# Values of the dilated groups projected with stationary weights and turned on TensorE

## The chip, the cores and the metric

The kernel runs on one core of one Trainium2 chip. The metric is the device time of one execution in microseconds (us), lower being better. Before the change it is 2150.77 us, the median of three runs (2149.27 to 2153.36).

## What is computed

The reference is a decoder trunk of two layers over 512 tokens of width 1024, all in float32. Each layer projects its input x once, runs three attention mixers (A: three groups of heads with dilated windows, B: a sliding window, C: latent attention), gates and merges them, and closes with a feed-forward part. The change concerns mixer A alone. Cut to it:

```
proj  = x @ w_in                          # x: 512 x 1024
a_qkv = proj[:, :4608].reshape(512, 3 groups, 3 (q, k, v), 8 heads, 64)
groups (window, dilation): (128, 1), (512, 4), (2048, 16)
for each group:
    tokens are regrouped by residue t mod dilation; within a residue
    each query attends to the keys of its causal band:
    p = softmax(q @ k.T / 8 + bias[distance])
    o = p @ v
o_a = the groups' outputs, weighted by their softmax denominators
```

Groups 1 and 2 are the dilated ones. The kernel sorts the tokens of both by residue modulo 4 (group 2's dilation of 16 is left to its bias table, which masks what is not a multiple of 16 apart), so four blocks of 128 tokens, one for each residue, take the place of the four blocks of 128 neighbours.

## The kernel before

Products are made from split numbers: every operand stands as a high and a low float32r part, and a product takes three matmuls into one bank (`mm3`, L170 to L173). The input stands transposed, as xT (xh, xl): model width on the partitions in eight chunks, the 512 tokens along the columns.

Mixer A of a layer is done in six jobs, `A_JOBS` = (0,0), (0,1), (0,2), (1,1), (1,2), (1,0): a half of the heads and a group. `project_a` makes a job's values, then for each of two pairs of heads (c) the query and the key projection: `o1` (L339) keeps 128 weight columns stationary and streams all 512 tokens, 8 chunks x 3 = 24 matmuls of 512 columns into a bank qkp. ACT copies the high part out and DVE subtracts it for the low part (`split_to`, L175). For a dilated group the copy regroups the columns by residue, and the key goes into a block-diagonal pair kh, kl, whose zero halves POOL sets (`block_diagonal`, L535). After each pair of heads four items of attention (one for a block of 128 queries) join the queue of `att`.

An item runs in three steps, each put into the program when `gap` finds that it is time for one: scores (scp), transposing the probabilities on TensorE (ptp, then pT), and values (op); its result goes by a row tile and a DMA issued on POOL to arow. `gap(time)` is called by the projections as they go on, and adds to a budget in proportion to the work left; the budget is capped at 4.

Values of the dilated groups come from `values_far` (L607), called in the job of group 1 for groups 1 and 2 of that half together: the stationary operand is every fourth token of xT, the moving one 512 weight columns (256 of either group), four residues into four banks at a time, three of tag mm and the only one of tag o; op uses that one too. All 96 matmuls stand before the first copy out; then four copies fill four slots vv, kept for both jobs, and one `gap(4 * UNIT)` follows.

Banks: three of tag mm (projections), two pt (transposes), two sc (scores), one o. Slots: the pool sp has 22 tiles of 4 KB a partition, shared by latT (three), vv, bias, q, kh, kl, pT, ct and others. Weights come through `Weights`: loads on the SP queue four ahead, splits (whi on ACT, wlo on DVE) two ahead. Within these rules a scheduler of the framework sets the order of the instructions on each engine when the program is built; an engine runs its own in that order, and a tile is taken when its last reader is through.

Of the kernel before, what the change touches and what calls it, by code (L numbers as in the profile page):

```python
# [12 lines left out]
F32 = mybir.dt.float32  # L13
F32R = mybir.dt.float32r
AF = mybir.ActivationFunctionType
# [5 lines left out]
P = 128  # L21
D = 1024
S = 512
KT = D // P
# [8 lines left out]
UNIT = 24 * 0.218  # L33
# [10 lines left out]
def dap(base, offset, dims):  # L44
    return bass.AP(tensor=base.tensor, offset=base.offset + offset, ap=[list(d) for d in dims])
# [88 lines left out]
def hybrid_trunk(ctx: ExitStack, tc: tile.TileContext, I, out):  # L134
    nc = tc.nc
# [13 lines left out]
    def mm_bank(name):  # L149
        return bank("mm", 3, name)  # L150

    def pt_bank(name):
        return bank("pt", 2, name)
# [4 lines left out]
    def o_bank(name):  # L158
        return bank("o", 1, name)
# [7 lines left out]
    def slot(name, dtype=F32):  # L167
        return sp.tile([P, 1024], dtype, name=name, tag="s")

    def mm3(o, lh, ll, rh, rl, start, stop):  # L170
        nc.tensor.matmul(o, lh, rh, start=start, stop=False)  # L171
        nc.tensor.matmul(o, lh, rl, start=False, stop=False)  # L172
        nc.tensor.matmul(o, ll, rh, start=False, stop=stop)  # L173

    def split_to(hi, lo, src, scale=None):  # L175
        if scale is None:
            nc.scalar.activation(hi, src, AF.Copy)  # L177
            nc.vector.tensor_tensor(lo, src, hi.bitcast(F32), ALU.subtract)  # L178
        else:
            nc.scalar.activation(hi, src, AF.Copy, scale=scale)  # L180
            nc.vector.scalar_tensor_tensor(lo, src, scale, hi.bitcast(F32), op0=ALU.mult, op1=ALU.subtract)  # L181


    specs = []
# [14 lines left out]
    def plan(l):  # L199
        w_in, r_in = I["w_in"], l * D  # L200

        def win(key, c0, n, k0=0, kts=KT, pool=None):
            col_chunk((l, key), w_in, r_in, D_IN, c0, n, k0=k0, kts=kts, pool=pool)

        for k in range(0, KT, 2):
            win(("lat", k), COL_CQ, 416, k, 2, sp if k < 4 else None)
        for j, (hf, g) in enumerate(A_JOBS):
            c0 = g * 1536 + hf * 256
            if g == 0:
                for k in (0, 4):  # L210
                    win((j, "v", k), c0 + 1024, 256, k, 4)
            elif g == 1:
                for k in range(0, KT, 2):
                    src = dap(w_in, r_in * D_IN + k * P * D_IN + c0 + 1024,
                              [[D_IN, P], [P * D_IN, 2], [1536, 2], [1, 256]])
                    pieces = [((lambda r, a=a: r.rearrange("p (k g n) -> p k g n", k=2, g=2)[:, a]), src[:, a])
                              for a in range(2)]
                    specs.append(((l, (j, "v", k)), 1024, pieces, None))
            for c in range(2):
                for nm, o in (("q", 0), ("k", 512)):  # L220
                    win((j, nm, c), c0 + o + c * P, P)
        win("bk", COL_BKV, P)
        win("bv", COL_BKV + P, P)
        for i in range(4):
            pieces = []
            for kv in range(2):
                src = dap(w_in, r_in * D_IN + COL_B + kv * 256 + i * 64, [[D_IN, P], [P * D_IN, KT], [1, 64]])
                pieces.append((lambda r, o=kv * 64: r.rearrange("p (k n) -> p k n", k=KT)[:, :, o:o + 64], src))
            specs.append(((l, "bq", i), 1024, pieces, None))
        for n in range(len(GATES) + GATE_LEAD):  # L230
            if n < len(GATES):
                i, f = GATES[n]
                win(("g", i, f), COL_G + i * D + f * P, P)
            if n >= GATE_LEAD:
                i, f = GATES[n - GATE_LEAD]
                if f % 2 == 0:
                    if i != 1:
                        col_chunk((l, "br", i, f), I["w_branch"], (l * 3 + i) * 512, D, f * P, 256, kts=4)
                        continue
                    pieces = []  # L240
                    for h in range(2):
                        src = dap(I["w_branch"], ((l * 3 + i) * 512 + h * 256) * D + f * P,
                                  [[D, 64], [64 * D, 4], [1, 256]])
                        pieces.append((lambda r, o=h * 64: r[o:o + 64].rearrange("p (k n) -> p k n", k=4), src))
                    specs.append(((l, "br", i, f), 1024, pieces, None))
        for c in range(2):
            for k in range(0, KT, 2):
                col_chunk((l, "wo", c, k), I["w_out"], l * D, D, c * 512, 512, k0=k, kts=2, pool=sp if c else None)
        for h0, h1 in HALVES:
            for f in range(h0, h1):  # L250
                col_chunk((l, "ug", f), I["w_ffn_up"], l * D, N_UP, f * P, P)
                col_chunk((l, "uv", f), I["w_ffn_up"], l * D, N_UP, D_FF + f * P, P)
            for c in range(2):
                for k in range(h0, h1, 2):
                    col_chunk((l, "dn", c, k), I["w_ffn_down"], l * D_FF, D, c * 512, 512, k0=k,
                              kts=min(2, h1 - k), pool=sp if (h1, c) == (KF, 1) and k >= h1 - 3 else None)
# [119 lines left out]
    for l in range(DEPTH):  # L376
# [172 lines left out]
        class JobA:  # L549
# [3 lines left out]
            def __init__(self, hf, g, c, bv, vv):  # L553
                self.hf, self.g, self.c, self.bv, self.vv = hf, g, c, bv, vv
                self.joint = g > 0
                self.vt, self.vh = (1, (g - 1) * 4 + 2 * c) if g else (2, 2 * c)

            def normalize(self, item, n):
                pass
# [47 lines left out]
        def values_far(l, j):  # L607


            pv = [mm_bank("vp") if r < 3 else o_bank("vp") for r in range(4)]  # L610
            for k in range(0, KT, 2):
                w = W.next((l, (j, "v", k)), 2, 512)
                for r in range(4):
                    for kk in range(2):
                        mm3(pv[r], xT[0][:, k + kk, r::4], xT[1][:, k + kk, r::4], w[0][:, kk, :], w[1][:, kk, :],
                            k + kk == 0, k + kk == KT - 1)
            vv = []
            for r in range(4):
                v = slot("vv", F32R).rearrange("p (h a d) -> p h a d", h=8, a=2)
                split_to(v[:, :, 0, :], v[:, :, 1, :], pv[r].rearrange("p (h d) -> p h d", h=8))  # L620
                vv.append(v[:, None])
            gap(4 * UNIT)
            return vv

        far = {}

        def project_a(l, j):

            hf, g = A_JOBS[j]
            if g == 0:  # L630
                vv = values_near(l, j)
            else:
                if g == 1:
                    far[hf] = values_far(l, j)
                vv = far[hf]
            if not tabs:
                make_tables()
            if j == 0:
# [462 lines left out]
```

## Time and profile before

| | |
|---|---|
| median of three runs | 2150.77 us (2149.27 to 2153.36) |
| profiled execution, its own time | 2152.71 us |
| its span, first to last instruction | 2151.0 us |
| TensorE (PE) busy | 2099.3 us, 98% |
| weight loads (PEld) | 1776.0 us, 83% |
| VectorE (DVE) | 1201.9 us, 56% |
| ScalarE (ACT) | 882.6 us, 41% |
| GpSimd (POOL) | 185.5 us, 9% |
| DMA | 220.32 MB, mean 102 GB/s |

Busy shares of TensorE are no measure of its pace: matmuls are pipelined, one that starts each 0.23 us is shown as lasting 0.39. The pace is read from the starts of neighbours in the timeline, and a slow stretch from idle time and from the granted clock. A layer takes half the span, and in each the dilated jobs follow the latent projections (from about 75 to 280 us in layer 0).

### The profile page before, as it was taken

The page shows a single profiled execution, that of the slowest core. Times are in us where ns is not written, and L with a number is a line of the kernel's source. Part 1 is how long each engine was busy: PE and PEld are TensorE (multiplying, and loading weights), DVE is VectorE, ACT ScalarE, POOL GpSimd, SP SyncE. Part 2 cuts the span into 40 slices and gives each one's busy share as a digit, 9 for nine tenths or more (in the row PEclk, how much of TensorE's full clock was granted, in tenths as well). Part 3 has the DMA queues.
Part 4 walks back from the last instruction along what each step waited for, and adds up shares of the span by engine and source line. Part 5 has one row for each costly group of instructions (what it writes and reads, how often), then busy time and mean ns, then how long its engine had stood idle before and what let it go on. Part 6 is the DMA issues. An engine that isn't in the chain of part 4 may idle for free. (4 is left out here: it accounts for less than half of the span.)

```text
span 2151.0 us, 29542 instructions
## 1 busy us (share of the span) xinstructions
PE 2099.3 (98%) x11074; PEld 1776.0 (83%) x11074; DVE 1201.9 (56%) x2585; ACT 882.6 (41%) x1874; POOL 185.5 (9%) x333
## 2 busy tenths in 40 slices
PE   8999999999999999999999989999999999999997
PEld 7888787788888888888888878878888888888886
DVE  4354556766646664366453546566665466644655
ACT  4343444555433343244233434445554324433431
POOL 1021211110000100000020212011010000000001
PEclk9999899999999999999999989999999999999999
DMA  6632433323236233333333233442222352333321
GB/s 183 201 89 82 121 93 116 87 68 97 62 111 195 69 98 93 103 98 93 117 110 87 85 86 106 100 126 77 74 76 76 109 185 73 95 95 101 98 93 64
DMA packets 291467, 220.32 MB, mean 102 GB/s; under 512 B 27914, under 2 KB 265435, under 8 KB 290812
## 3 DMA queue, kind: packets, MB, share of 16 engines
q1 hardware_dynamic: 284860, 203.55, 32.7%
q0 software_dynamic: 6464, 14.89, 2.3%
q8 instruction: 87, 1.43, 0.3%
q14 instruction: 56, 0.46, 0.1%
HBM read 201.38 MB, written 22.26 MB: 104 GB/s over the span
## 5 line engine op out<-in xcount | busy, mean ns | idle before, releaser
L77 DVE TENSOR_TENSOR wlo<-wraw,whi 128x1024 fp32r<-128x1024 f32 (+2 forms) x316 | 380.0, 1204 | 431.6 <-ACT whi L76 429.1
L76 ACT ACTIVATE whi<-wraw 128x1024 fp32r<-128x1024 f32 (+2 forms) x316 | 329.0, 1044 | 454.2 <-PE dnp L172 119.0
L172 PE MATMUL up<-xl,whi 128*128 128x512 f32 (+1 forms) x768 | 285.3, 372 | 0.4
L171 PE MATMUL up<-xh,whi 128*128 128x512 f32 (+1 forms) x768 | 284.2, 372 | 0.7 <-ACT xh L328 0.5
L173 PE MATMUL up<-xh,wlo 128*128 128x512 f32 (+1 forms) x768 | 284.5, 371 | 0.0
L171 PE MATMUL qkp<-xh,whi 128*128 128x512 f32 x464 | 188.3, 406 | 6.8 <-DVE q L181 6.7
L173 PE MATMUL qkp<-xh,wlo 128*128 128x512 f32 x464 | 187.3, 404 | 0.0
L172 PE MATMUL qkp<-xl,whi 128*128 128x512 f32 x464 | 187.3, 404 | 0.0
L171 PEld LDWEIGHTS up<-xh,whi 128*128 128x128 f32 x768 | 144.0, 188 | 26.7 <-ACT xh L328 1.6
L172 PEld LDWEIGHTS up<-xl,whi 128*128 128x128 f32 x768 | 144.7, 188 | 25.9 <-DVE xl L333 1.2
L173 PEld LDWEIGHTS up<-xh,wlo 128*128 128x128 f32 x768 | 144.5, 188 | 24.9
L171 PE MATMUL gp<-xh,whi 128*128 128x512 f32 x384 | 154.7, 403 | 0.7 <-ACT gs L886 0.7
L172 PE MATMUL gp<-xl,whi 128*128 128x512 f32 x384 | 153.2, 399 | 0.0
L173 PE MATMUL gp<-xh,wlo 128*128 128x512 f32 x384 | 152.2, 396 | 0.0
L493 ACT ACTIVATE sb<-sb,row 128x128 f32<-128x128 f32 (+1 forms) x192 | 81.0, 422 | 140.1 <-DVE row L490 134.1
L172 PE MATMUL dnp<-wlo,hT 128*128 128x512 f32 x352 | 136.9, 389 | 0.0
L173 PE MATMUL dnp<-whi,hT 128*128 128x512 f32 x352 | 136.8, 389 | 0.0
L171 PE MATMUL dnp<-whi,hT 128*128 128x512 f32 x352 | 135.6, 389 | 0.0
L177 ACT ACTIVATE pT<-ptp 128x512 fp32r<-128x512 f32 (+1 forms) x176 | 82.0, 477 | 116.3 <-PE ptp L504 114.7
L178 DVE TENSOR_TENSOR pT<-ptp,pT 128x512 fp32r<-128x512 f32 (+1 forms) x176 | 93.6, 540 | 53.1 <-ACT pT L177 52.5
L490 DVE CUSTOM_DVE_ANT_0 sb<-scp,bias 128x128 f32<-128x128 f32 (+1 forms) x192 | 55.7, 320 | 116.7 <-DMA arow<-row 98.7
L171 PEld LDWEIGHTS qkp<-xh,whi 128*128 128x128 f32 x464 | 89.4, 193 | 24.0 <-DVE q L181 7.9
(301 smaller groups left out, 4354.1 us busy)
## 6 DMA issues: line engine op xcount, KB each, us to landing
wraw<-in_w_in_dram SPq DMA_DIRECT2D x108, 512.0 KB, 4.0
wraw<-in_w_ffn_up_dram SPq DMA_DIRECT2D x88, 512.0 KB, 4.0
wraw<-in_w_ffn_down_dram SPq DMA_DIRECT2D x40, 512.0 KB, 3.8
wraw<-in_w_in_dram SPq DMA_DIRECT2D x48, 256.0 KB, 3.6
wraw<-in_w_branch_dram SPq DMA_DIRECT2D x16, 512.0 KB, 3.5
wraw<-in_w_out_dram SPq DMA_DIRECT2D x16, 512.0 KB, 6.7
arow<-row POOLq DMA_DIRECT2D x96, 66.0 KB, 1.9
ct<-arow SPq DMA_DIRECT2D x16, 396.0 KB, 3.5
```

Of the source, the lines that this page charges most:

```text
L76: nc.scalar.activation(hi[:, :n], raw[:, :n], AF.Copy)
L77: nc.vector.tensor_tensor(lo[:, :n], raw[:, :n], hi[:, :n].bitcast(F32), ALU.subtract)
L171: nc.tensor.matmul(o, lh, rh, start=start, stop=False)
L172: nc.tensor.matmul(o, lh, rl, start=False, stop=False)
L173: nc.tensor.matmul(o, ll, rh, start=False, stop=stop)
L177: nc.scalar.activation(hi, src, AF.Copy)
L178: nc.vector.tensor_tensor(lo, src, hi.bitcast(F32), ALU.subtract)
L490: nc.vector.tensor_tensor_reduce(v[:, h, :], pp[h], j.bias(h, nk), -j.scale, j.floor(h), ALU.add, ALU.min, self.st[:, h:h + 1])
L493: nc.scalar.activation(v[:, h, :], v[:, h, :], AF.Exp, bias=self.st[:, h:h + 1], scale=-1.0, accum_out=self.st[:, 2 + h:3 + h])
```

## The change

`values_far` is called once for each job of a dilated group (four a layer instead of two) and makes the values of that group alone. For each pair of heads it calls `o1` with 128 value columns stationary and all 512 tokens moving, into one mm bank; ACT copies that bank out by residue into v_T (tag w2); TensorE turns the four blocks of 128 into a bank vtp of tag pt; and `split_to` copies them in two parts into two slots vv. `gap` is called within `o1` and after the copy. The weights are loaded in the form of the query and key chunks.

```
-            elif g == 1:
-                for k in range(0, KT, 2):
-                    src = dap(w_in, r_in * D_IN + k * P * D_IN + c0 + 1024,
-                              [[D_IN, P], [P * D_IN, 2], [1536, 2], [1, 256]])
...
+            else:
+                for c in range(2):
+                    win((j, "v", c), c0 + 1024 + c * P, P)
...
-                self.vt, self.vh = (1, (g - 1) * 4 + 2 * c) if g else (2, 2 * c)
+                self.vt, self.vh = 2, 2 * c
...
-            pv = [mm_bank("vp") if r < 3 else o_bank("vp") for r in range(4)]
-            for k in range(0, KT, 2):
-                w = W.next((l, (j, "v", k)), 2, 512)
+            vv = [slot("vv", F32R).rearrange("p (t h a d) -> p t h a d", t=2, h=4, a=2) for _ in range(2)]
+            for c in range(2):
+                p = mm_bank("vp")
+                o1(p, W.next((l, (j, "v", c)), KT, P), 0, xT, gap)
+                v_T = tp.tile([P, S], F32, name="v_T", tag="w2", bufs=4)
+                nc.scalar.activation(v_T.rearrange("p (r i) -> p r i", r=4), p.rearrange("p (i r) -> p r i", r=4),
+                                     AF.Copy)
+                gap(UNIT / 2)
+                p = pt_bank("vtp")
                 for r in range(4):
-                    for kk in range(2):
-                        mm3(pv[r], xT[0][:, k + kk, r::4], xT[1][:, k + kk, r::4], w[0][:, kk, :], w[1][:, kk, :],
-                            k + kk == 0, k + kk == KT - 1)
-            vv = []
-            for r in range(4):
-                v = slot("vv", F32R).rearrange("p (h a d) -> p h a d", h=8, a=2)
-                split_to(v[:, :, 0, :], v[:, :, 1, :], pv[r].rearrange("p (h d) -> p h d", h=8))
-                vv.append(v[:, None])
-            gap(4 * UNIT)
+                    nc.tensor.transpose(p[:, r * P:(r + 1) * P], v_T[:, r * P:(r + 1) * P], ident)
+                pv = p.rearrange("p (t h d) -> p t h d", t=4, h=2)
+                for a in range(2):
+                    v = vv[a][:, :, 2 * c:2 * c + 2]
+                    split_to(v[:, :, :, 0, :], v[:, :, :, 1, :], pv[:, 2 * a:2 * a + 2])
             return vv
...
-            if g == 0:
-                vv = values_near(l, j)
-            else:
-                if g == 1:
-                    far[hf] = values_far(l, j)
-                vv = far[hf]
+            vv = values_far(l, j) if g else values_near(l, j)
```

The scheduler gives the engines another order all through the attention part. Three places of job 3 of layer 0, the job (1,1), show it. On ACT, before, around the copy of its first query projection (q_1932; kh_1988 is its first key, pT and sb belong to items of job 2, whi to weights):

```order
L177 ACTIVATE pT_1850<-ptp_1847 128x256
L493 ACTIVATE sb_1830,row_1831<-sb_1830,row_1831 128x128 x2
L177 ACTIVATE pT_1873<-ptp_1870 128x256
L493 ACTIVATE sb_1853,row_1854<-sb_1853,row_1854 128x128 x2
L493 ACTIVATE sb_1876,row_1877<-sb_1876,row_1877 128x128 x2
L177 ACTIVATE pT_1917<-ptp_1914 128x256
L180 ACTIVATE q_1932<-qkp_1894 128x512
L177 ACTIVATE pT_1945<-ptp_1942 128x256
L76 ACTIVATE whi_2145<-wraw_1998 128x1024
L177 ACTIVATE kh_1988<-qkp_1954 64x512
```

On ACT, now, around the same copy (q_1897; v_T_1830 is the second value projection of the job, vv_1663 and vv_1664 are its value slots):

```order
L611 ACTIVATE v_T_1830<-vp_1776 128x512
L177 ACTIVATE vv_1664<-vtp_1767 128x2x2x64
L489 ACTIVATE sb_1757,row_1758<-sb_1757,row_1758 128x128 x2
L177 ACTIVATE pT_1805<-ptp_1802 128x256
L76 ACTIVATE whi_1915<-wraw_1777 128x1024
L489 ACTIVATE sb_1808,row_1809<-sb_1808,row_1809 128x128 x2
L177 ACTIVATE pT_1842<-ptp_1839 128x256
L180 ACTIVATE q_1897<-qkp_1872 128x512
L177 ACTIVATE vv_1663<-vtp_1855 128x2x2x64
```

The query's copy stood behind item steps alone; it now stands among steps of the job's own values.

On POOL, before, around the zeroing of the job's two key tiles (kh_1988, kh_2131; the rows stored are those of job 2's last items):

```order
L588 DMA arow0_419<-row_1831 128x132
L588 DMA arow0_419<-row_1854 128x132
L588 DMA arow0_419<-row_1877 128x132
L540 MEMSET kh_1988 64x512
L541 MEMSET kh_1988 64x512
L540 MEMSET kl_1991 64x512
L541 MEMSET kl_1991 64x512
L540 MEMSET kh_2131 64x512
```

On POOL, now, around the zeroing of the same job's first key tile (kh_1957):

```order
L584 DMA arow0_419<-row_1735 128x132
L536 MEMSET kh_1957 64x512
L537 MEMSET kh_1957 64x512
L536 MEMSET kl_1960 64x512
L537 MEMSET kl_1960 64x512
L584 DMA arow0_419<-row_1758 128x132
L584 DMA arow0_419<-row_1809 128x132
L584 DMA arow0_419<-row_1846 128x132
L536 MEMSET kh_2109 64x512
```

The zeroing of the first key moved from behind the last store of job 2 to before its last three.

On PE, before, behind the third projection of the job (qkp_2004); of the 35 rows of attention that follow before the next projection matmul, the first eleven:

```order
L173 MATMUL qkp_2004<-xh_114,wlo_1951 128x512
L522 MATMUL op_1794<-vv_894,pT_1781 128x128
L523 MATMUL op_1794<-vv_894,pT_1781 128x128
L522 MATMUL op_1794<-vv_894,pT_1781 128x128
L523 MATMUL op_1794<-vv_894,pT_1781 128x128
L171 MATMUL scp_1855<-kh_1579,q_1498 128x256
L172 MATMUL scp_1855<-kl_1582,q_1498 128x256
L173 MATMUL scp_1855<-kh_1579,q_1498 128x256
L504 MATMUL ptp_1847<-ident_78,sb_1807 128x128 x2
L522 MATMUL op_1817<-vv_897,pT_1804 128x128
L523 MATMUL op_1817<-vv_897,pT_1804 128x128
L522 MATMUL op_1817<-vv_897,pT_1804 128x128
```

On PE, now, within the job's first key projection (qkp_1919), around the second batch of value transposes (vtp_1855):

```order
L172 MATMUL qkp_1919<-xl_115,whi_1779 128x512
L173 MATMUL qkp_1919<-xh_114,wlo_1780 128x512
L518 MATMUL op_1795<-vv_1215,pT_1754 128x128
L519 MATMUL op_1795<-vv_1215,pT_1754 128x128
L518 MATMUL op_1795<-vv_1215,pT_1754 128x128
L519 MATMUL op_1795<-vv_1215,pT_1754 128x128
L616 MATMUL vtp_1855<-ident_78,v_T_1830 128x128 x4
L171 MATMUL qkp_1919<-xh_114,whi_1779 128x512
L172 MATMUL qkp_1919<-xl_115,whi_1779 128x512
```

Attention stood in one long row there; it now stands in short ones between projection matmuls, with the new transposes among them.

## Rows read from the trace of the kernel before

**Rows 1.** The page: busy us of an engine; granted TensorE clock, tenths, forty slices

```profile
PE 2099.3 (98%) x11074; PEld 1776.0 (83%) x11074; DVE 1201.9 (56%) x2585; ACT 882.6 (41%) x1874; POOL 185.5 (9%) x333
...
PEclk9999899999999999999999989999999999999999
```

**Rows 2.** Busy time by stretch: length, then each engine's busy us, clock, DMA

```profile
102.57:163.38 60.81, 60.81 (x341) 50.99 (x340) 32.72 (x86) 28.95 (x75) 12.43 (x23) 1.00 0.32 91
209.55:239.09 29.54, 22.08 (x81) 17.21 (x80) 13.88 (x46) 10.13 (x30) 7.91 (x15) 0.71 0.32 100
1270.31:1302.54 32.23, 22.84 (x81) 17.79 (x80) 14.71 (x49) 10.13 (x30) 7.91 (x15) 0.68 0.38 117
```

**Rows 3.** Groups on PE, 209.55 to 239.09: busy us, mean ns, idle before

```profile
L171 PE MATMUL qkp<-xh,whi 128*128 128x512 f32 x13 | 7.0, 541 | 3.4 <-DVE q L181 3.4
...
L522 PE MATMUL op<-vv,pT 128*128 128x128 f32 x14 | 5.0, 365 | 2.3 <-DVE row L585 1.8 <-ACT pT L177 0.5
...
L504 PE MATMUL ptp<-ident,sb 128*128 128x128 f32 x8 | 3.0, 418 | 0.8 <-ACT sb L493 0.8
L171 PE MATMUL scp<-kh,q 128*128 128x256 f32 x2 | 0.9, 454 | 1.0 <-DVE row L490 1.0
```

**Rows 4.** Timeline of PE, undisturbed: start us, us shown, instruction, count

```profile
60.57 0.39 PE L171 MATMUL qkp<-xh,whi 128*128 128x512 f32 x1
...
70.31 0.39 PE L172 MATMUL qkp<-xl,whi 128*128 128x512 f32 x1
...
85.80 0.40 PE L171 MATMUL vp<-whi,xh 128*128 128x512 f32 x1
...
100.84 0.40 PE L173 MATMUL vp<-whi,xl 128*128 128x512 f32 x1
...
102.16 0.66 PE L504 MATMUL ptp<-ident,sb 128*128 128x128 f32 x4
102.57 0.48 PE L171 MATMUL qkp<-xh,whi 128*128 128x512 f32 x1
102.89 0.40 PE L172 MATMUL qkp<-xl,whi 128*128 128x512 f32 x1
...
114.09 0.28 PE L523 MATMUL op<-vv,pT 128*128 128x128 f32 x1
...
114.76 0.28 PE L523 MATMUL op<-vv,pT 128*128 128x128 f32 x1
...
340.90 0.60 PE L720 MATMUL vtp<-ident,v_T 128*128 128x128 f32 x4
341.44 0.62 PE L488 MATMUL scp<-k,q 64*128 64x256 f32 x3
```

**Rows 5.** Timeline of PE, ACT and POOL in job 3 of layer 0

```profile
179.99 0.27 PE L523 MATMUL op<-vv,pT 128*128 128x128 f32 x1
...
198.71 0.22 PE L522 MATMUL op<-vv,pT 128*128 128x128 f32 x1
...
221.31 0.58 ACT L180 ACTIVATE q<-qkp 128x512 fp32r<-128x512 f32 x1
...
231.57 0.52 POOL L540 MEMSET kh<- 64x512 f32 x1
...
234.34 0.80 PE L171 MATMUL qkp<-xh,whi 128*128 128x512 f32 x1 [3.37 <-DVE q L181]
...
237.48 0.39 PE L172 MATMUL qkp<-xl,whi 128*128 128x512 f32 x1
```

**Rows 6.** Weight loads of the strided tokens, 85.8 to 101: busy us, mean ns

```profile
L172 PEld LDWEIGHTS vp<-wlo,xh 128*128 128x128 f32 x22 | 6.8, 310 | 0.0
```

**Rows 7.** Copies out: groups by shape, and one tile's instructions (min/median/max ns)

```profile
L177 ACT ACTIVATE vv<-vp 128x512 fp32r<-128x512 f32 x24 | 14.2, 592 | 10.5 <-PE vp L173 10.4
...
L716 ACT ACTIVATE v_T<-vp x2: 581/581/581, 322.9 to 1386.4; 128x512 f32<-128x512 f32 x2
```

**Rows 8.** Busy time by stretch, as in rows 2, behind the dilated jobs

```profile
340.00:430.00 90.00, 86.73 (x543) 69.05 (x544) 64.18 (x224) 48.69 (x145) 11.63 (x21) 1.00 0.35 101
1402.00:1495.00 93.00, 90.36 (x570) 72.33 (x569) 66.59 (x236) 51.02 (x153) 12.22 (x22) 1.00 0.35 102
```

More of the change, by code (lines that the diff above doesn't have):

```diff
@@ L211, in plan @@
                     win((j, "v", k), c0 + 1024, 256, k, 4)
-            elif g == 1:
-                for k in range(0, KT, 2):
-                    src = dap(w_in, r_in * D_IN + k * P * D_IN + c0 + 1024,
-                              [[D_IN, P], [P * D_IN, 2], [1536, 2], [1, 256]])
-                    pieces = [((lambda r, a=a: r.rearrange("p (k g n) -> p k g n", k=2, g=2)[:, a]), src[:, a])
-                              for a in range(2)]
-                    specs.append(((l, (j, "v", k)), 1024, pieces, None))
+            else:
+                for c in range(2):
+                    win((j, "v", c), c0 + 1024 + c * P, P)
             for c in range(2):
@@ L607, in values_far @@
         def values_far(l, j):
-            pv = [mm_bank("vp") if r < 3 else o_bank("vp") for r in range(4)]
-            for k in range(0, KT, 2):
-                w = W.next((l, (j, "v", k)), 2, 512)
-                for r in range(4):
-                    for kk in range(2):
-                        mm3(pv[r], xT[0][:, k + kk, r::4], xT[1][:, k + kk, r::4], w[0][:, kk, :], w[1][:, kk, :],
-                            k + kk == 0, k + kk == KT - 1)
-            vv = []
-            for r in range(4):
-                v = slot("vv", F32R).rearrange("p (h a d) -> p h a d", h=8, a=2)
-                split_to(v[:, :, 0, :], v[:, :, 1, :], pv[r].rearrange("p (h d) -> p h d", h=8))
-                vv.append(v[:, None])
-            gap(4 * UNIT)
+            vv = [slot("vv", F32R).rearrange("p (t h a d) -> p t h a d", t=2, h=4, a=2) for _ in range(2)]
[7 more added lines that the diff above has]
+                p = pt_bank("vtp")
+                for r in range(4):
+                    nc.tensor.transpose(p[:, r * P:(r + 1) * P], v_T[:, r * P:(r + 1) * P], ident)
[3 more added lines that the diff above has]
+                    split_to(v[:, :, :, 0, :], v[:, :, :, 1, :], pv[:, 2 * a:2 * a + 2])
             return vv
-        far = {}
         def project_a(l, j):
             hf, g = A_JOBS[j]
-            if g == 0:
-                vv = values_near(l, j)
-            else:
-                if g == 1:
-                    far[hf] = values_far(l, j)
-                vv = far[hf]
+            vv = values_far(l, j) if g else values_near(l, j)
             if not tabs:
```

## The prediction

> **What bounds the kernel now.** I read the page first: its engine table and its forty slices. TensorE is busy for 2099.3 of 2151.0 us, and its clock is at full speed in nearly every slice [rows 1]. So time can go in two ways only: fewer or shorter TensorE instructions, or fewer waits on TensorE. What DVE, ACT or the DMA queues gain is worth nothing by itself.
>
> Next I looked for the stretches in which TensorE is slower than its own pace. Almost all of the dilated stage is clean: from 102.57 to 163.38 us it is busy for every one of the 60.81 us at a granted clock of 1.00. Two stretches are not, one in each layer, both in job 3, the first dilated job of the second half of the heads: 209.55 to 239.09 (busy 22.08 of 29.54 us, clock 0.71) and 1270.31 to 1302.54 (22.84 of 32.23, clock 0.68) [rows 2]. How much is lost there follows from what ran. The first of them holds 39 projection matmuls (three lines of 13), 28 value matmuls (two lines of 14), 8 transposes and 6 score matmuls (three lines of 2) [rows 3], 81 in all; the other has the same count [rows 2]. Undisturbed, 44 projection matmuls start between 60.57 and 70.31, so one takes 9.74 / 43 = 0.2265 us; a value matmul takes (114.76 - 114.09) / 6 = 0.112; four transposes with the slower start behind them take 0.41 + (0.32 - 0.23) = 0.50, or 0.54 where a score matmul follows [rows 4]. With score matmuls at the value matmuls' pace that is 39 x 0.2265 + 34 x 0.112 + 8 x 0.125 = 13.6 us of work. So 29.5 - 13.6 = 15.9 us are lost in layer 0 and 32.2 - 13.6 = 18.6 in layer 1, together 34.5, part as idle time and part as a halved clock behind it.
>
> Why there? The chain of releases shows it. The value matmuls of attention stop at 179.99 and come back at 198.71 [rows 5]: in between the joint value projection of both dilated groups holds the one bank of tag o as its fourth output, and nothing of attention can finish. After that, TensorE runs its three projections, all three mm banks are full, and they can't be emptied: the first query copy runs on ACT at 221.31, and the memsets of the first key tile on POOL at 231.57 [rows 5]. These wait for slots of the pool sp. It has 22; three hold latT, and at this point the values hold eight (four of the half before, still read by job 2, and four of the new half), so eleven are left for biases, queries, keys and transposed probabilities. They come free only as job 2's attention items finish, one after another. The order shows the same: ACT's copy of q_1932 stands behind seven item steps of job 2, and POOL's memsets behind the last store of that job. The last of it is a wait of 3.37 us at 234.34, and after it seven steps take 3.14 us, 0.449 each, twice the pace: the clock is at the lower of its two levels, 1.2 instead of 2.4 GHz, after TensorE has stood still [rows 5].
>
> **The change part by part.**
>
> *Pace of the value matmuls.* Their count stays: 4 residues x 8 x 3 = 96 of 512 columns for each half before, 2 groups x 2 x 24 = 96 after; with two halves and two layers 384. Before, the stationary operand is every fourth token of xT; 65 such matmuls start from 85.80 to 100.84, which is 15.04 / 64 = 0.235 each [rows 4]. After, they have the form of the query projections, 0.2265. That gives 384 x 0.0085 = -3.3 us. A load of the strided weights takes 310 ns [rows 6], longer than a matmul's step, and yet the step is 0.235. The Trainium skill, SBUF — State Buffer (section Door 1: The DMA port swizzle), says that a stride of four fp32 elements reaches a new line of 16 bytes at each element and is slow; the long load agrees with it. Had the load set the step, the gain would be 384 x (0.310 - 0.2265) = -32 us; the steps on the rows decide for -3.3.
>
> *Transposes.* Sixteen batches of four (8 per layer) are new, on TensorE, at 0.50 to 0.54 each [rows 4]: 16 x 0.51 = +8.2 us, nothing hides it. Its floor is four times the value matmuls' 0.112, or +7.2.
>
> *Copies.* Sixteen ACT copies of 512 columns at 0.59 and as many DVE subtractions (16 of the 24 in [rows 7]; the other eight are group 0) are replaced by sixteen copies by residue and 32 pairs of 256 columns. Contiguous copies of this kind take 0.581 [rows 7]. The one by residue reads PSUM with a stride of four, as the query copy at 221.31 does, which takes 0.58 [rows 5]. If each of the 32 took as much as a copy of 512, ACT would gain 48 x 0.59 - 16 x 0.59 = 19 us over both layers. In the clean stretch ACT is busy for 28.95 of 60.81 us and DVE for 32.72 [rows 2], so this stays hidden at 0; without that cover it would be all of 19. One more step is on TensorE's path, the wait of a batch for its v_T; see the rivals. Weight loads: the same bytes in 512 KB pieces of the q and k form, on the same SP queue in the same places; 0.
>
> *Slots and banks.* Values of a job now take two slots and die with it: seven of 22 instead of eleven at job 3. The value projection takes one mm bank at a time and never the o bank, so attention goes on beside it. In the new order q_1897 is copied out among item steps, the memsets stand before the last stores of job 2, and no run of attention without projections is left there on TensorE; each batch of transposes stands at least 13 projection matmuls and 18 attention instructions behind the end of its source, 13 x 0.2265 + 18 x 0.112 = 5.0 us. I take the whole 34.5 us as gone. What is late next is nothing that the order shows: TensorE's own work, at 1.00 as in the clean stretch. The bounds are 0 (the stall stays) and -34.5.
>
> Sum: 8.2 - 3.3 - 34.5 = -29.6. The profiled execution took 2152.7 us, 1.9 above the median of 2150.8; 2152.7 - 29.6 = 2123.1, and by the median 2121.
>
> **The rivals.**
> *Half of it stays.* The four slots turn out too few, or another in-order queue takes over: say the row tiles (four) whose stores POOL issues. For it: the smaller waits in the stretch are waits of item on item, on the row reduction of DVE and on the transposed probabilities of ACT [rows 3]. Against it: in the clean stretch the same items run at the same rate beside projections. 2121 + 17 = 2138.
> *It does not do what it says for the stall.* If the values' slots and the o bank are not the cause, only the first two terms are left: +8.2 - 3.3 = +4.9, so 2155.7. Against it stands that the stall comes in job 3 alone, where values of both halves are held, and in both layers.
> *Transposes that wait* (the other side). TensorE works in order: if ACT comes late with v_T, the batch stands and the projection behind it too. One such wait costs as the last one did, 3.37 idle and 3.14 - 7 x 0.2265 = 1.55 for the low clock, 4.9 us. If all sixteen wait, +79: 2200. It decides from six of sixteen on (29.6 / 4.9). It needs ACT to be more than those 5.0 us late; in the clean stretch ACT is half idle.
> *The transposes lower the clock.* If the clock fell after each batch, about 1.55 us would be lost each time [rows 5], 16 x 1.55 = +25, so 2146. The clean stretch has items with transposes throughout, at 1.00 [rows 2]. The Trainium skill, TensorE: Matmul & The Clock Gate (Part 4: PE-mode transpose), says that transposes don't count as activity for the clock; by that rule this rival would come true where they stand in a row, but four of them last 0.5 us.
> *More than the two stretches.* Attention that is done earlier leaves less for the end of the dilated and the window part, where TensorE idles 3.3 us from 340 to 430 and 2.6 from 1402 to 1495 [rows 8]. If that goes too: 2115.
>
> **How the numbers follow.** Forecast 0.62, half stays 0.16, more 0.12, the stall unchanged 0.04, transposes that wait 0.03, clock 0.03. Predicted is 2121. The range, 2107 (the case of more, with some room) to 2141 (half stays, with some room), leaves out the last three cases and the misses around the first three, a tenth to two tenths. A measurement of this kernel can tell about 0.2%, 4.3 us, from no change. Faster by more than that are forecast, half, more and half of the clock case, 0.91; the other half, and a part of the waiting transposes, within it, 0.03; slower the rest, 0.06.
>
> **What the changed profile would show.** Right: no wait in TensorE's list on the query copy's subtraction, a granted clock near 1.00 in job 3 of both layers, its busy share there full; value matmuls stepping at 0.227; 72 transposes into vtp instead of 8, about 0.5 us per four; ACT's copies of q and the key memsets within a few us of the end of their projection. Wrong: idle time before vtp that ends with ACT's v_T, a stretch of clock below 1.00 anywhere from 160 to 240 us, or a wait for a bank at its old place.

## The result, and the profile after

The changed kernel takes 2120.84 us (median of 4 runs, 2120.16 to 2121.85) beside 2151.07 of the kernel before: a ratio of 0.9863, 95% interval 0.9851 to 0.9875, or 29.5 us less. Its profiled execution took 2121.85 us, its span is 2120.0. The two lines of the page that answer to [rows 1], engine times and granted clock:

```profile
PE 2084.7 (98%) x11138; PEld 1745.7 (82%) x11138; DVE 1198.1 (57%) x2601; ACT 889.9 (42%) x1906; POOL 185.0 (9%) x333
PEclk9999999999999999999999999999999999999999
```

TensorE idles for 2120.0 - 2084.7 = 35.3 us instead of 51.7, and is busy for 14.6 us less although it has 64 instructions more; the halved clock of job 3 is gone. The windows view shows it, here of before and then of after, four stretches of layer 0 (busy time and instructions of each engine, granted clock, DMA share, GB/s); job 3 is in the second, and in after job 4 begins there too, at about 210 us:

```profile
core 0: us, PE busy (x) PEld busy (x) DVE busy (x) ACT busy (x) POOL busy (x), PEclk, DMA share, GB/s
70.00:155.00 85.00, 85.00 (x450) 73.57 (x449) 40.62 (x96) 37.70 (x87) 11.35 (x21) 1.00 0.44 120
155.00:240.00 85.00, 77.54 (x353) 67.90 (x353) 38.70 (x112) 31.90 (x85) 14.29 (x27) 0.90 0.33 96
240.00:335.00 95.00, 95.00 (x547) 80.94 (x546) 55.91 (x171) 46.10 (x131) 15.45 (x29) 1.00 0.38 96
335.00:400.00 65.00, 63.45 (x386) 50.02 (x385) 47.81 (x175) 34.96 (x107) 9.57 (x17) 1.00 0.45 136
```

```profile
70.00:155.00 85.00, 85.00 (x472) 69.83 (x471) 42.59 (x117) 41.33 (x107) 12.97 (x24) 1.00 0.42 121
155.00:240.00 85.00, 84.76 (x448) 71.63 (x447) 49.18 (x149) 39.51 (x109) 15.90 (x30) 1.00 0.40 117
240.00:335.00 95.00, 93.01 (x523) 76.58 (x522) 48.23 (x135) 43.73 (x118) 13.83 (x26) 1.00 0.35 91
335.00:400.00 65.00, 64.53 (x389) 50.71 (x388) 47.91 (x180) 34.28 (x106) 8.49 (x15) 1.00 0.40 118
```

From 155 to 240 us TensorE starts 448 instead of 353 instructions at a clock of 1.00 instead of 0.90 and idles 0.24 instead of 7.46 us. From 240 to 335 it now idles 2.0 us, where it idled none. TensorE's list of waits in the whole of after (us in total, times, the longest) begins with the loading of x and the latent part; the waits inside the dilated jobs are short ones on the row reduction:

```profile
PE xtp L321 <- DMA xin<-in_x_dram: 5.2, 2, 4.8
PE latp L171 <- ACT xh L324: 4.0, 4, 2.9
PE scp L171 <- DVE row L486: 3.5, 4, 1.1
```

The wait on the subtraction of the query copy (6.7 us in two pieces before) isn't in it. The new operations, all sixteen batches of values, by the view of the tile vtp and the groups of ACT (times of one in ns: least, median, longest; in the last line the mean):

```profile
L616 PE MATMUL vtp<-ident,v_T x64: 272/273/296, 88.4 to 1278.0; 128*128 128x128 f32 x64
L177 ACT ACTIVATE vv<-vtp x32: 360/384/386, 89.1 to 1284.2; 128x256 fp32r<-128x256 f32 x32
```

```profile
L611 ACT ACTIVATE v_T<-vp 128x512 f32<-128x512 f32 x16 | 9.4, 585 | 0.0
```

**Where the 31 us went.** For each TensorE instruction I took the time to the next one's start and subtracted the median of its own form in the same execution. What is over, summed by stretch (us from the first xtp of the layer; layer 0 / layer 1; bp is the first merge matmul, wop the first of the output projection):

| stretch | before | after | difference |
|---|---|---|---|
| 70 to 155 (first two dilated jobs) | 1.5 / 2.2 | 1.6 / 1.7 | -0.4 |
| 155 to 240 (job 3; in after also job 4 from about 210) | 18.6 / 21.1 | 4.0 / 5.2 | -30.5 |
| 240 to 335 (job 4 or its end, last job) | 5.4 / 5.7 | 9.6 / 9.6 | +8.1 |
| 335 to bp (window part, gates, rest of mixer A) | 9.0 / 7.8 | 4.7 / 3.8 | -8.3 |
| bp to wop | 10.8 / 11.9 | 9.3 / 10.4 | -3.0 |

With 6.8 us more in the steps of the transposes (72 take 7.9 us, 8 took 1.1) and 384 x (0.237 - 0.227) = 3.8 less in the value matmuls (medians of their steps) that is -31.1, the difference of the spans (31.0). How forms are grouped for the median moves a difference by up to 2 us; its sign and the order of the large ones stay, except that the first is too small for a sign. Landmarks that need no median agree: from the start of its layer the first bp comes at 386.3 and 379.4 us instead of 399.2 and 394.9, together 28.4 earlier, and the first wop at 644.4 and 638.7 instead of 658.8 and 655.6, together 31.3 earlier.

### The profile page after: what moved, and what is told of

It is laid out like the page before. It is cut to its first block, busy times and chain, and to the rows that moved or that the text cites. A ratio compares the mean times of both kernels' runs of the same rounds, so it can differ in the third digit from the quotient of the medians.

```text
span 2120.0 us, 29699 instructions
## 1 busy us (share of the span) xinstructions
PE 2084.7 (98%) x11138; PEld 1745.7 (82%) x11138; DVE 1198.1 (57%) x2601; ACT 889.9 (42%) x1906; POOL 185.0 (9%) x333
## 5 line engine op out<-in xcount | busy, mean ns | idle before, releaser
L173 PEld LDWEIGHTS qkp<-xh,wlo 128*128 128x128 f32 x464 | 87.3, 188 | 17.9 <-issue 0.4
```

## The experiments

The prediction names two causes for job 3: the slots that the values hold, and the o bank. A third came up with the first runs: the changed form calls `gap` inside the value projection, the old one only once behind it. The budget's cap of 4 then drops what is over; counted from the code and not from a trace, that is 4.8 of the 9.3 that the call adds at job 3. Ratios are to the kernel before on the same chip; "against after" is a difference of ratios times 2151 us.

| kernel | gap within | bank of attention held | value slots at job 3 | median us | ratio (95%) |
|---|---|---|---|---|---|
| before | no | o | 8 | 2151 to 2153 | 1 |
| e2_no_o_bank | no | pt | 8 | 2149.01 | 0.9986 (0.9975 to 0.9996) |
| e2c_spread | yes | pt | 8 | 2160.71 | 1.0052 (1.0034 to 1.0069) |
| e12_two_banks | yes | none | 8 | 2127.84 | 0.9885 (0.9870 to 0.9901) |
| e3_joint | yes | none | 6 | 2126.35 | 0.9880 (0.9867 to 0.9894) |
| after | yes | none | 4 | 2120.84 | 0.9863 (0.9851 to 0.9875) |
| e10_gap_after | no | none | 4 | 2142.67 | 0.9961 (0.9948 to 0.9974) |
| e9_after_o | yes | o | 4 | 2151.10 | 0.9999 (0.9987 to 1.0010) |
| e7_slots18 | yes | none | 4 of 18 | 2140.43 | 0.9941 (0.9926 to 0.9956) |

**The o bank taken away from the joint projection (e2_no_o_bank).** Edit of before:

```
-            pv = [mm_bank("vp") if r < 3 else o_bank("vp") for r in range(4)]
+            pv = [mm_bank("vp") if r < 3 else pt_bank("vp") for r in range(4)]
```

> The kernel before with one change: the fourth output of the joint value projection stands in a bank of tag pt instead of the one bank of tag o. The values still hold eight slots at job 3, as before. If the slots of the pool sp make the stall of job 3 (theory S), it stays: about 2151 us, within 6, with query copies and key memsets late and a halved clock behind them at 210 to 240 us. If it is the bank held by the projection, which keeps attention from finishing anything (theory O), most of the 34.5 us go: 2117 to 2125. If both are needed, something between, about 2135.

It gained 3 us, so theory O as I had put it falls. But pt is a bank that attention needs too, so this run alone can't tell which bank is held from a bank being held. Waits of TensorE from 155 to 240 us, and the windows row (of an execution of 2145.49 us, among the shortest of the ten):

```profile
PE qkp L171 <- DVE q L181: 3.0, 1, 3.0
PE op L522 <- DVE row L585: 1.6, 1, 1.6
```

```profile
155.00:240.00 85.00, 79.64 (x381) 70.69 (x380) 41.74 (x122) 33.29 (x87) 14.88 (x28) 0.94 0.38 106
```

Both kinds of wait are still there: on the copy of a projection, and inside the items' own chain.

**More slots held, in the new form (e3_joint).** Edit of after: at the job of group 1 `values_far` is run for both groups and the second result kept.

```
...
+            if g == 1:
+                far[hf, 1], far[hf, 2] = [values_far(l, j, a) for a in range(2)]
+            vv = far[hf, g] if g else values_near(l, j)
```

> The changed kernel (weights stationary, transposes, no use of the o bank), but the values of both dilated groups are made at the job of the first of them and kept for two jobs, so that they hold eight slots at job 3 as in the kernel before. Theory S: the stall comes back, 2121 + 34.5 = about 2155. Theory O: it stays away, 2119 to 2125. Both needed: 2121 to 2138.

Its text says eight slots; it is six, since here each group has its own two, and those of group 1 of the half before are free again at job 3 (eight are held in e12_two_banks, below). Nearly all of the gain stays; making both groups at once, with two slots more held, costs 0.0017 x 2151 = 3.7 us, and the two intervals overlap. The waits from 155 to 240 us:

```profile
PE scp L171 <- DVE row L486: 2.4, 2, 1.7
PE scp L172 <- DVE kl L178: 1.6, 1, 1.6
PE qkp L171 <- DVE q L181: 1.5, 1, 1.5
```

The wait on the copy of q is back, half as long as in before and e2, and one on kl stands beside it. From 155 to 240 us it has 12.4 and 14.2 us over the median steps (layers 0 and 1; 4.0 and 5.2 in after), and most of that is won again behind it: the first wop comes 644.3 and 641.6 us after the start of its layer, in after 644.4 and 638.7. So of 17.4 us lost there 2.8 are left at the first wop.

**Gap and bank, in both forms.** The next four kernels are about these two. e2c_spread is e2 with the gap spread:

```
             for k in range(0, KT, 2):
...
+                gap(UNIT)
...
-            gap(4 * UNIT)
```

> The kernel before, with the fourth output bank taken from tag pt as in e2_no_o_bank, and with the one gap(4 * UNIT) behind the joint value projection replaced by a gap(UNIT) after each of its four weight chunks. Theory G: what the changed form gains is that gap is called within the value projection, so that attention items go on beside it and less of them is left for job 3 and for the end of the dilated part (the budget is capped at 4, and what is over is lost). Then most of the gain comes here: 2121 - 8.2 + 3.3 = 2116 to 2130, and idle time before the gate part falls. If spacing is not it and the eight slots held at job 3 are, the stall stays as in e2_no_o_bank: about 2149.

It is 11 us slower than before. With the gap spread, items are put in while the projection still holds one of the two pt banks. Its waits from 155 to 240 us, and the windows row:

```profile
PE op L522 <- ACT pT L177: 4.0, 4, 2.6
PE op L522 <- DVE row L585: 1.2, 1, 1.2
```

```profile
155.00:240.00 85.00, 78.49 (x363) 68.40 (x362) 44.86 (x129) 32.05 (x87) 15.93 (x30) 0.90 0.35 101
```

The value steps now wait for transposed probabilities. e12_two_banks keeps the old form (every fourth token stationary, no transposes, eight slots), but holds two mm banks at a time only, calls `gap` within, and loads and splits the weights twice for it:

```
...
+            for half in range(2):
+                pv = [mm_bank("vp") for r in range(2)]
                 for k in range(0, KT, 2):
-                    w = W.next((l, (j, "v", k)), 2, 512)
+                    w = W.next((l, (j, "v", half, k)), 2, 512)
...
+                    gap(UNIT / 2)
...
-            gap(4 * UNIT)
```

> The kernel before in its own form (every fourth token stationary, 512 columns, both groups together, eight slots held, no transposes), but two residues at a time into two banks of tag mm, so that no bank that attention uses is held, with a gap(UNIT / 2) after each of eight weight chunks (the weights are loaded and split twice for it) and no gap(4 * UNIT). Theory GB (the changed form gains because attention is handed out during the value projection and finds all its banks free; transposes and stationary weights are only a way to that): nearly all of the gain comes here, 2121 - 6 for the transposes + 5 for the eight slots (e3_joint) + 3 to 8 for the strided operand = 2123 to 2129. If the changed form itself is needed: 2140 to 2151.

It has 24.7 of the 29.5 us, with all eight slots held, without one value transpose in mixer A and without the weights as stationary operand. So theory S falls too, as the main cause. Its waits in the same stretch are on copies first:

```profile
PE qkp L171 <- DVE vv L178: 2.4, 1, 2.4
PE scp L171 <- ACT kh L177: 1.2, 1, 1.2
```

From the other side, e10_gap_after takes the gap out of the changed form:

```
-                o1(p, W.next((l, (j, "v", c)), KT, P), 0, xT, gap)
+                o1(p, W.next((l, (j, "v", c)), KT, P), 0, xT, lambda time: None)
...
-                gap(UNIT / 2)
...
+            gap(2 * UNIT)
             return vv
```

> The changed kernel, with the value projection calling no gap: neither within its 24 matmuls nor after the copy to v_T; one gap(2 * UNIT) stands behind it, as one of 4 stood behind the joint one. Two slots per job, the o bank free, as in the changed kernel. Theory G: the gain is lost for the most part, 2140 to 2151, and a batch of transposes may wait for its v_T. If slots and bank are the cause, it stays at 2121 to 2125.

and e9_after_o leaves the gap and lays the value projection into the o bank:

```
-                p = mm_bank("vp")
+                p = o_bank("vp")
```

> The changed kernel, with the value projections put out into the one bank of tag o instead of a bank of tag mm, so that attention's value step waits for each of them, while slots, transposes and gap stay as changed. Theory O (the o bank held stops attention): a part of the stall comes back, 2130 to 2155, with idle time of TensorE before op or scp in job 3. If the bank is of no account: 2121, within 4.

The first loses 21.1 us, the second all 29.3. The windows row and the longest waits from 155 to 240 us, of e10:

```profile
155.00:240.00 85.00, 81.00 (x408) 68.15 (x407) 50.64 (x158) 39.88 (x115) 18.54 (x35) 0.94 0.39 112
```

```profile
PE op L518 <- DVE row L581: 1.8, 1, 1.8
PE ptp L500 <- ACT sb L489: 1.5, 1, 1.5
```

and of e9:

```profile
155.00:240.00 85.00, 78.39 (x374) 64.30 (x373) 43.53 (x145) 37.72 (x106) 17.35 (x33) 0.92 0.32 94
```

```profile
PE op L518 <- DVE row L581: 3.2, 4, 1.3
PE op L518 <- ACT v_T L611: 1.1, 1, 1.1
```

Neither has a wait on a copy of q or k among its longest, and in e10 no batch of transposes waits for its v_T. What waits is one step of an item for the step before it (op for the row of the last item, ptp for the exponentials): items that couldn't go on beside the projection follow each other without projections in between. The timeline of TensorE in e9 shows the hole:

```profile
201.05 0.27 PE L519 MATMUL op<-vv,pT 128*128 128x128 f32 x1
...
208.74 0.39 PE L173 MATMUL vp<-xh,wlo 128*128 128x512 f32 x1
208.97 0.39 PE L171 MATMUL qkp<-xh,whi 128*128 128x512 f32 x1
...
214.18 0.39 PE L173 MATMUL qkp<-xh,wlo 128*128 128x512 f32 x1
214.41 0.22 PE L518 MATMUL op<-vv,pT 128*128 128x128 f32 x1
```

No value step between 201.05 and 214.41, over a whole value projection and a query or key projection; in after a value step stands in the midst of a value projection:

```profile
212.31 0.39 PE L171 MATMUL vp<-xh,whi 128*128 128x512 f32 x1
212.54 0.22 PE L518 MATMUL op<-vv,pT 128*128 128x128 f32 x1
...
212.93 0.45 PE L172 MATMUL vp<-xl,whi 128*128 128x512 f32 x1
```

So nearly all of the gain needs two things together: gap within the projection (without it, in e10, 8.4 us are left), and no bank held that an item needs (else e9, e2c: none). That they suffice for most of it in either form, e3 and e12 show. The budget's cap isn't what counts: counted from the code it drops nothing in e10, and e10 loses 21.1 us all the same.

**Fewer slots for everybody (e7_slots18).** After with `bufs=18` for sp instead of 22.

> The changed kernel with 18 instead of 22 tiles in the pool sp: at job 3 eleven are left beside latT and the values, as many as in the kernel before. If the slots were the larger part of the stall (the prediction's first named cause), job 3 stands still again, with waits on query and key copies from 200 to 240 us and some 25 us lost: 2145. By e3_joint, where eight slots held cost 5 us, it is 2124 to 2130; more is possible from the gate and merge parts, which use the same pool, and is then read outside of the dilated jobs.

It is 16.8 us slower than after, but most of it not in job 3. Until the first wop of each layer its profiled execution has lost 2.3 and 2.5 us; the rest is lost in the merge, from that wop to the next part's first transpose: 48.1 us in each layer instead of 39.0 (some 2.7 us in all come back behind it). Its longest wait of TensorE:

```profile
PE xtp L321 <- DVE x L360: 13.6, 5, 5.2
```

It isn't in the list of after. With as few slots left at job 3 as before the change (eleven), 4.8 us are lost up to the merge, one execution against one, near the 3.7 of e3. Its longest wait from 155 to 240 us is one of 1.2 on the exponentials, and none is on a copy; so what else, beside slots, makes the copies late in e2, e3 and e12 stays open.

**The transposes (e5_twice_turned).** After, with `for r in (0, 1, 2, 3) * 2` around the value transposes.

> The changed kernel with each batch's four value transposes done twice into the same bank: 64 more. By the prediction's term, 16 x 0.51, it is 8.2 us slower than the changed kernel (its floor 7.2): 2121 + 8 = about 2129. By the mean step of the transposes in the trace of the changed kernel (72 take 7.9 us with the waits among them; 16 in the clean stretch take 1.4) 64 x 0.09 = 5.8: about 2127. If transposes lower the clock, a granted clock under 0.99 and over 2135.

The ratio is 0.9880 (0.9865 to 0.9894), 3.7 us more than after, with the two intervals overlapping. The steps of its 136 transposes sum to 14.0 us, 6.1 more than after's. Its clock is lower, but for the end of the span, in one place of each layer only; in layer 0:

```profile
380.00:400.00 20.00, 15.83 (x95) 12.74 (x93) 11.65 (x45) 8.65 (x32) 1.34 (x3) 0.91 0.19 68
```

and that follows a wait of 3.4 us (2.4 in layer 1), where the last items of mixer A are through and their output is loaded again, far from any value transpose. In the dilated jobs, with eight in a row, it is at 1.00. The wait, and the windows row of job 3:

```profile
PE otp L453 <- DVE bst L691: 5.9, 2, 3.4
```

```profile
155.00:240.00 85.00, 84.34 (x453) 71.85 (x452) 49.87 (x151) 39.47 (x108) 15.90 (x30) 1.00 0.39 115
```

**The strided operand (e6_neighbours, e4_per_job_tokens).** e6 is before with `r * P:(r + 1) * P` in place of `r::4` as the stationary tokens; it leaves out the regrouping by residue, so its values are those of other tokens, and it serves for the time alone.

> The kernel before, where only the stationary operand of the joint value projection is another: 128 neighbouring tokens instead of every fourth one, so the values of the dilated groups are taken of other tokens than the reference takes. Instructions, order, banks and slots are those of before. By the steps of before (0.235 strided, 0.2265 for the contiguous form) 384 x 0.0085 = 3.3 us less: about 2148, with loads of 190 instead of 310 ns. If a value projection doesn't care, 2151; if the strided loads cost more than the steps show, under 2145.

Its ratio is 0.9964 (0.9950 to 0.9978): 7.7 us less, 4.7 to 10.8. The loads and the steps:

```profile
L173 PEld LDWEIGHTS vp<-whi,xl 128*128 128x128 f32 x23 | 4.3, 188 | 1.0
```

(66 matmuls from 85 to 100 us; 188 ns a load instead of 310, [rows 6]). The median step falls from 0.237 to 0.227 us, which is 3.8 us for 384; all steps of 512-column value matmuls together fall from 106.0 to 100.8, 5.2 us, since those beside attention gain more. e4, an edit of after, has the strided tokens in 256 columns, one group at a time, by the form of group 0:

```
-        def values_near(l, j):
+        def values_near(l, j, far=False):
...
-                ts_ = slice(t * P, (t + 1) * P)
+                ts_ = slice(t, None, 4) if far else slice(t * P, (t + 1) * P)
...
-            vv = values_far(l, j) if g else values_near(l, j)
+            vv = values_near(l, j, g > 0)
```

> The values projected as in the kernel before, with every fourth token stationary and no transposes, but for one group at a time: 768 matmuls of 256 columns instead of 384 of 512, two banks of tag mm, two slots that live for one job. Both theories of the stall let it go here. What it measures is whether the per-job form needs the transposes: at the step of group 0's 256-column value matmuls in the kernel before, 0.120 us, they take 768 x 0.120 = 92.2 us, against 384 x 0.2265 + 8.2 = 95.2 in the changed kernel, so about 2118 us. If the loads of strided weights (310 ns each in the kernel before) set the step, 768 x (0.310 - 0.120) = 146 us more: about 2264.

The ratio is 1.0169 (1.0155 to 1.0183), 2188.65 us. The timeline has contiguous tokens first, strided ones after, 256 columns both:

```profile
46.07 0.28 PE L171 MATMUL vp<-whi,xh 128*128 128x256 f32 x1
46.19 0.28 PE L172 MATMUL vp<-wlo,xh 128*128 128x256 f32 x1
...
86.59 0.40 PE L172 MATMUL vp<-wlo,xh 128*128 128x256 f32 x1
86.82 0.40 PE L173 MATMUL vp<-whi,xl 128*128 128x256 f32 x1
```

0.120 and 0.233 us a step (medians): at 256 columns the strided load sets it. At 512 columns the step is 0.237 strided and 0.227 contiguous (e6), so these only just cover the load. 768 x (0.233 - 0.120) = 87 us were to come on top of 2118; 71 did. Of the other 16 us, 10 are in the steps of the query and key projections (327.4 us in sum instead of 337.5 in after); why was not tried. So stationary weights with transposes are the right form once the projection is per job.

**Two tries to go on from the o bank.** e11_two_o is after with two o banks and two mm banks; e14_op_mm is after with every fourth item's value step in an mm bank:

```
-        return bank("mm", 3, name)
+        return bank("mm", 2, name)
...
-        return bank("o", 1, name)
+        return bank("o", 2, name)
...
```

```
-                o = o_bank("op")
+                o = (o_bank if j.direct or t % 4 else mm_bank)("op")
```

> The changed kernel with two banks of tag o and two of tag mm instead of one and three (the second merge and feed-forward blocks take two and two). If the one o bank, which e9_after_o shows to be decisive when it is held, limits attention in the changed kernel too, the scp waits on the row reduction shrink and it is faster: 2112 to 2118. If two mm banks make the projections wait for their copies instead, slower: 2125 to 2140. If neither, 2121.

> The changed kernel, with the value step of every fourth item of mixers A put into a bank of tag mm instead of the one of tag o; banks are as in the changed kernel, three mm and one o. In e11_two_o the dilated part was 4.5 us (layer 0) and 6.5 us (layer 1) shorter up to the first gate projection, and the part with the latent items longer, where only two mm banks were left. If the o bank still limits attention in the changed kernel, the first is kept without the second: 2121 - 11 = 2110, and not over 2117. If the shorter dilated part was only work moved to later, 2119 to 2123; if the shared rotation of the mm banks holds up projections, 2124 to 2135.

Neither is faster than after: 0.9884 (0.9867 to 0.9901) and 0.9892 (0.9875 to 0.9908), 4.5 and 6.2 us slower, with intervals that overlap or touch that of after. In e11 the way to the first bp is shorter (383.1 and 374.1 us from the layer's start, after 386.3 and 379.4), but it is lost again behind it: 264.4 and 263.5 us from there to the first wop, after 258.1 and 259.3. That the two mm banks left do this was expected and not tested by itself. e14 should have kept the first and didn't: 388.2 and 380.8. Both have a wait that after hasn't, in e11 and e14:

```profile
PE op L518 <- ACT pT L177: 6.0, 4, 2.9
```

```profile
PE op L518 <- ACT pT L177: 12.0, 6, 3.9
```

With more banks for them, value steps stand so soon behind their transposes that they wait for ACT's copies. No version here beats the changed kernel.

## Why the prediction held, step by step

The time was right, within 0.2 us by the median, and that close a fit is luck: the largest term came out right as a sum of parts that were not foreseen, and of the two causes named for it the one that carried most of the reasoning was the lesser.

*The stall of job 3: -34.5 forecast, -34.1 by the table above, all rows together.* From 155 to 240 us 30.5 went, and 9.2 stayed in small pieces. Behind it 8.1 came back from 240 to 335 us, beside the end of job 4 and the last job; in these stretches the trace names waits of 1.4 us only (0.8 of a score on the row reduction, twice 0.3 on kl), the rest is in short delays that I haven't taken apart. And 8.3 went before bp. So the rival of more than the two stretches came true for its half, and "what is late next is nothing that the order shows" was wrong by as much; the two cancel.

*Its cause.* The step that failed is the one that reads the late copies of q_1932 and its key as the cause of the stall: "these wait for slots of the pool sp". The row of the wait behind them names the longest single wait, but slots are worth a few us: 3.7 in e3 (with both groups made at once), 4.8 in e7. e12 with all eight held is 4.7 from after; it also pays for the strided operand (3.8 by the steps) and saves the transposes (some 7), so up to 8 could be the slots'. 21 to 29 us come back with no more slots than in after, in e10 and e9. Late copies are not even gone: in after the second query projection of job 3 has its last matmul at 203.43, and ACT copies it out 12 us later, while TensorE works on at full pace:

```profile
203.43 0.39 PE L173 MATMUL qkp<-xh,wlo 128*128 128x512 f32 x1
```

```profile
215.51 0.60 ACT L180 ACTIVATE q<-qkp 128x512 fp32r<-128x512 f32 x1
```

The o bank, which the prediction names as well (no value step between 179.99 and 198.71 [rows 5], and "attention goes on beside it" in the new form), was the better clue, and giving it back alone was not enough (e2, where pt takes its place; e10): I had left out that no gap is called within the old projection, which stands in the code and which no row shows. With both given, 2126 to 2128 us are reached with six or eight slots, in the new form and in the old.

*That the change is about stationary weights and transposes.* They are a way to make room, not what gains: e12 has 24.7 of the 29.5 us without them.

*Transposes: +8.2 forecast, floor 7.2.* 64 more took 6.8 us of steps, and twice as many took 6.1 more; in time 3.7. These steps leave out that the matmul behind a batch starts later, and hold a wait of 0.80 us of a score that has nothing to do with them (at 1279.12 us). An undisturbed batch in after, among matmuls of 0.23:

```profile
88.41 0.60 PE L616 MATMUL vtp<-ident,v_T 128*128 128x128 f32 x4
88.77 0.48 PE L173 MATMUL vp<-xh,wlo 128*128 128x512 f32 x1
89.09 0.39 PE L171 MATMUL vp<-xh,whi 128*128 128x512 f32 x1
```

It costs 0.36 + (0.32 - 0.23) = 0.45, sixteen of them 7.2, which is the floor; my row [rows 4] had 0.41 in place of the 0.36. The rival by which transposes would lower the clock (the Trainium skill, TensorE: Matmul & The Clock Gate, Part 4: PE-mode transpose) didn't come: 1.00 in every window with value transposes, in e5 with eight in a row.

*Pace of the value matmuls: -3.3 forecast.* By e6 7.7, 4.7 to 10.8, of which the steps show 5.2. "Had the load set the step" was answered wrongly: it does set it, only at some 0.235 and not at the 0.310 that a load lasts, so at 512 columns just above the matmul's own 0.2265. The stride therefore matters here, by 4% of a step at 512 columns and by a factor of 1.9 at 256. The rule that each access which crosses to a new line of 16 bytes pays a penalty (the Trainium skill, SBUF — State Buffer, Door 1: The DMA port swizzle) agrees with that; with one stride tried, no run shows that the line is the reason. Of this gain the changed kernel shows less: its value matmuls are mixed with attention now, and their steps sum to 103.3, 2.7 less than before.

*Copies: 0.* Right. TensorE waits nowhere for a v_T. The copies add 9.4 + 32 x 0.379 - 16 x 0.592 = 12 us on ACT, not 19, since copies of 256 columns take 379 ns where I had counted 590; the engine as a whole is busy for 7.3 us more.

*What it said the profile would show* is there for the clock, the busy share, the step of the value matmuls and the wait on the query copy's subtraction. It was wrong on the copies of q and the key memsets, which were to come within a few us of the end of their projection and come up to 12 us behind it in job 3 (above). And four waits of scores on row reductions, 0.8 to 1.1 us each, remain beside job 4 and the last job, where none were foreseen.

## What to carry to other kernels

When one stretch stands still in the middle of a well-filled pipeline, look also for what was kept from running before it: here a long block that calls no hand-over and holds a buffer that the other stream needs. Both had to go; either alone brought 8 us of 30 at best, and 11 lost at worst. The longest wait tells who came last, not what it costs: test a resource by giving back or taking away that one alone (here the slots, a few us of the 34 that had been laid to them and the bank).

## What was not expected of the hardware

- A load of 128 x 128 strided by four float32 lasts 310 ns, and yet matmuls with such loads start each 0.233 us: hidden behind a matmul of 512 columns (0.227) but for 3 to 4%, and not behind one of 256 (0.120). e4 took 71 us more than expected, for the most part by this.
- ACT reading PSUM with a stride of four took 585 ns for 512 columns (v_T, L611); contiguous copies take 581 to 592 [rows 7].
- Four float32 transposes cost 0.45 us of TensorE's time although one is shown as lasting 273 ns, and a second set of them cost less in time (3.7 us, with intervals that overlap) than in its own steps (6.1): the order around them changed too.
